# One encoder block on one core: gelu and decay steps in fewer wide VectorE instructions, the first convolution tap on ScalarE, every third low part of the weights on VectorE

## Chip, cores and metric

One core of a Trainium2 chip runs the whole block. The metric is device time in microseconds (us), the median of three runs. The names of the engines in the profile: PE is TensorE (PEld its weight loads), DVE is VectorE, ACT is ScalarE, POOL is GpSimd, SP is SyncE, which here only issues transfers.

## What is computed

The input is 256 positions of 2048 float32 features, and there is one layer. It has a mixer and a retrieval over single-neuron experts:

```python
n = rms_norm(h)
z = n @ w_in                                  # 2048 -> 4 x 1024: xr, gr, gu, gv
xc = conv(xr)                                 # depthwise, 4 taps: y = b + sum_k x[t+k] * w[k]
for each direction:                           # RG-LRU, 8 heads of 128 channels
    r, i  = sigmoid(xc @ w_a + b_a), sigmoid(xc @ w_x + b_x)
    log_a = -8 * softplus(-lam) * r
    a, u  = exp(log_a), sqrt(-expm1(2 * log_a)) * (i * xc)
    h_t   = a_t * h_{t-1} + u_t               # a scan over the 256 positions
A = gelu(gr) * (h_forward + h_backward)
B = gelu(gu) * (w_s[head] @ layer_norm(gelu(gv)) + b_s)
h = h + concat(A, B) @ w_out
h = h + peer(rms_norm(h))                     # queries, two top 16, 128 of 16384 experts a position
out = rms_norm(h)
```

Gelu is the tanh form, x (1 + tanh(GA x + GB x^3)) / 2.

## The kernel before

**Steps.** The three projections (w_in, w_out and w_q, all 2048 deep) are worked off in 256 steps in one loop, 128 for w_in, 64 for w_out and 64 for w_q. A step takes 128 rows by 512 columns of weights. The weight is split into a rounded part hi and a rest lo, and three products stand for one float32 product: hi by hi, hi by the input's lo, lo by the input's hi. `stage_h` (line 279) does the split: ScalarE casts `hi` (L286), and VectorE or GpSimd subtracts to give `lo` (L289). A counter `nl` chooses: every fourth on VectorE, except in a part of the last projection, the others on GpSimd. There are five buffers of hi and of lo. Splitting runs LH = 4 steps ahead of the matmuls. A step has 12 matmuls of 256 columns where the result stands feature by feature (w_in's groups for xr, gr and gu, and w_q), and 6 matmuls of 512 columns otherwise (w_in's groups for gv, and w_out). In this text steps are counted from 0; the groups of 16 steps of w_in come in the order xr, xr, gv, gv, gr, gr, gu, gu.

**Lanes.** All other work of the mixer stands in generators. Behind every step's matmuls, `slices` (line 80) takes one piece, up to the next yield, of the first generator in each of three lanes (`bg3`, `bg`, `bg2`). So the program's order, and with it each engine's queue, is fixed when the program is made: a yield is one step. For steps 128 to 139 slices is called twice, and `reload_x` at step 140 drains the lanes. Lane `bg3` reads finished accumulators (`lru`, `evac`), lane `bg` holds `lru2(0)` and then `lru2(1)`, lane `bg2` holds the gates in order: gate_v(0), gate_v(1), gate_r(0), gate_r(1), gate_u(0), gate_u(1). `gate_r(g)` waits, in program order, until `lru2(g)` has marked itself done.

**lru2 (line 357).** For four heads (g = 0 or 1): the convolution, per head one tensor_scalar for tap 0 with the bias (L365) and three scalar_tensor_tensor (L369), two yields a head. Then for each direction, called a decay pass here: the gate matmuls (L381) and two Tanh a head (L386, L387), Exp and Tanh a head (L394, L395), and on 1024 columns, for all four heads at once: L399 (input gate), L401 (clamp of the negated tanh), Sqrt on ScalarE (L403), twice L405 and L407 (a product and an affine step), a GpSimd product (L409), L411, and four scans (L416 or L418). After the second direction GpSimd adds the two results (L423).

**gelu2 (line 446).** Square on ScalarE (L449), a tensor_scalar (L451), a product (L453), Tanh on ScalarE (L455). It is used six times on 1024 columns, by gate_v (then L498 and the layer norm: L510 to L522), gate_r (L462, L467, then `put_y`: casts yh and rests yl, L339 and L341) and gate_u (matmuls L535 and L537 that mix the positions, L540, L544, put_y).

**What follows.** The product with w_out needs yh and yl of all lanes. After the queries come the scores, the choice of experts, and two gathers on GpSimd's queue of 256 rows each (u, then v), with the dot products (L913) and the weighted sum (L959).

Of the kernel before, what the change touches and what calls it, by code (L numbers as in the profile page):

```python
# [11 lines left out]
AF = mybir.ActivationFunctionType  # L12
OP = mybir.AluOpType
# [5 lines left out]
T = 256  # L19
# [22 lines left out]
GA = math.sqrt(2.0 / math.pi)  # L42
GB = 0.044715 * GA


def build(tc, x, mix_norm_g, w_in, conv_w, conv_b, lru_w_a, lru_b_a, lru_w_x, lru_b_x,
# [3 lines left out]
    vec, act, pool, pe = nc.vector, nc.scalar, nc.gpsimd, nc.tensor  # L50
# [19 lines left out]
    def psm(shape, name):  # L70
        return ps.tile(shape, F32, name=name, tag="m", bufs=4)
# [34 lines left out]
    G1, G2, CW, CB, BA, BX, LAM = 0, 16, 32, 64, 72, 88, 104  # L106
# [9 lines left out]
    prm = pa.tile([P, P], F32, name="prm")  # L116
# [5 lines left out]
    def wait(n):  # L122
        for _ in range(n):
            yield
# [145 lines left out]
    def load_next():  # L270
        if nload[0] < len(srcs):
            s = srcs[nload[0]]
            nload[0] += 1
            s.raw = stm.tile([P, 1024], F32, name="raw", bufs=RB)
            s.load(s.raw)

    nl = [0]

    def stage_h(s):
        if s.ahead:  # L280
            s.ahead()
        q = s.q % 2
        s.h = stm.tile([P, 512], F32R, name="hi", bufs=HB)
        s.l = stm.tile([P, 512], F32R, name="lo", bufs=HB)
        a, h, l = s.src.raw[:, q * 512:(q + 1) * 512], s.h, s.l
        act.copy(h, a)  # L286
        nl[0] += 1
        e = vec if nl[0] % 4 == 0 and not o_end + 14 <= nl[0] < o_end + 42 else pool
        e.tensor_tensor(l, a, h.bitcast(F32), op=OP.subtract)  # L289
        if s.last:  # L290
            load_next()
# [65 lines left out]
    def lru2(g, xp):  # L357
        wg = p1.tile([P, 2, 2, 4, P], F32, name="wg")
        for d in range(2):
            for n, w in enumerate((lru_w_a, lru_w_x)):  # L360
                act.dma_start(wg[:, d, n], w[0, d, 4 * g:4 * g + 4].rearrange("h c e -> c h e"))
        for b in range(4):
            hb = 4 * g + b
            o = xc[:, hb]
            vec.tensor_scalar(o, xp[:, b, 0:T], prm[:, CW + hb:CW + hb + 1], prm[:, CB + hb:CB + hb + 1],  # L365
                              op0=OP.mult, op1=OP.add)
            for k in range(1, 4):
                c = CW + 8 * k + hb
                vec.scalar_tensor_tensor(o, xp[:, b, k:k + T], prm[:, c:c + 1], o, op0=OP.mult, op1=OP.add)  # L369
                if k == 1:  # L370
                    yield
            yield
        for d in range(2):
            tr = p1.tile([P, 4, T], F32, name="ltr")
            ti = p1.tile([P, 4, T], F32, name="lti")
            zs = []
            for b in range(4 + WP):
                if b < 4:
                    z = psm([P, 2, T], "gz")
                    for n in range(2):  # L380
                        mm(z[:, n], lhsT=wg[:, d, n, b], rhs=xc[:, 4 * g + b], start=True, stop=True)  # L381
                    zs.append(z)
                if b >= WP:
                    z = zs[b - WP]
                    j = d * 8 + 4 * g + b - WP
                    act.activation(tr[:, b - WP], z[:, 0], AF.Tanh, scale=0.5, bias=drv[:, HBA + j:HBA + j + 1])  # L386
                    act.activation(ti[:, b - WP], z[:, 1], AF.Tanh, scale=0.5, bias=drv[:, HBX + j:HBX + j + 1])  # L387
                yield
            a = p1.tile([P, 4, T], F32, name="lom")
            s = p1.tile([P, 4, T], F32, name="ls")  # L390
            for b in range(4):
                j = d * 8 + 4 * g + b
                cj, ej = drv[:, C4 + j:C4 + j + 1], drv[:, C8 + j:C8 + j + 1]
                act.activation(a[:, b], tr[:, b], AF.Exp, scale=ej, bias=ej)  # L394
                act.activation(tr[:, b], tr[:, b], AF.Tanh, scale=cj, bias=cj)  # L395
                if b % 2:
                    yield

            vec.scalar_tensor_tensor(ti, ti, 1.0, xc[:, 4 * g:4 * g + 4], op0=OP.add, op1=OP.mult)  # L399
            yield  # L400
            vec.tensor_scalar(tr, tr, -1.0, 0.0, op0=OP.mult, op1=OP.max)  # L401
            yield
            act.activation(s, tr, AF.Sqrt)  # L403
            for n in range(2):
                vec.scalar_tensor_tensor(a, a, 1.0, tr, op0=OP.add, op1=OP.mult)  # L405
                yield
                vec.tensor_scalar(a, a, -1.0, 1.0, op0=OP.mult, op1=OP.add)  # L407
                yield
            pool.tensor_tensor(ti, ti, s, op=OP.mult)  # L409
            yield from wait(3)  # L410
            vec.scalar_tensor_tensor(ti, a, 1.0, ti, op0=OP.add, op1=OP.mult)  # L411
            yield
            for b in range(4):
                hb = 4 * g + b
                if d == 0:
                    vec.tensor_tensor_scan(hs[:, hb], a[:, b], ti[:, b], 0.0, op0=OP.mult, op1=OP.add)  # L416
                else:
                    vec.tensor_tensor_scan(tr[:, b][:, ::-1], a[:, b][:, ::-1], ti[:, b][:, ::-1], 0.0,  # L418
                                           op0=OP.mult, op1=OP.add)
                if b % 2:  # L420
                    yield
            if d == 1:
                pool.tensor_tensor(hs[:, 4 * g:4 * g + 4], hs[:, 4 * g:4 * g + 4], tr, op=OP.add)  # L423
                done.add(g)
            yield
# [20 lines left out]
    def gelu2(xx):  # L446

        t = p1.tile([P, 1024], F32, name="g2")
        act.activation(t, xx, AF.Square)  # L449
        yield  # L450
        vec.tensor_scalar(t, t, GB, GA, op0=OP.mult, op1=OP.add)  # L451
        yield
        vec.tensor_tensor(t, t, xx, op=OP.mult)  # L453
        yield
        act.activation(t, t, AF.Tanh)  # L455
        yield from wait(2)
        return t

    def gate_r(g, xx):
        t = yield from gelu2(xx)  # L460
        y2 = p1.tile([P, 1024], F32, name="g3")
        vec.scalar_tensor_tensor(y2, t, 1.0, xx, op0=OP.add, op1=OP.mult)  # L462
        yield
        while g not in done:
            yield
        yv = y2.rearrange("p (b t) -> p b t", b=4)
        vec.scalar_tensor_tensor(yv, yv, 0.25, hs[:, 4 * g:4 * g + 4], op0=OP.mult, op1=OP.mult)  # L467
        yield
        yield from put_y(4 * g, yv, 4)
# [528 lines left out]
    o_end = z_end + 4 * 16  # L998
# [23 lines left out]
    for n in range(N + LT):  # L1022
# [6 lines left out]
        s = steps[c]  # L1029
# [62 lines left out]
```

## Time and profile before

| what | value |
|---|---|
| three runs | 1688.69, 1699.1, 1694.52 us; median 1694.52 |
| the profiled execution | 1699.92 us, its span 1698.2 us, mean TensorE clock granted 0.747 |
| busy over the span | PE 59%, PEld 43%, DVE 77%, ACT 39%, POOL 61% |
| low parts (L289) | POOL x199, 297.0 us; DVE x57, 64.7 us |
| chain that ended last, by engine | DMA 34%, DVE 22%, PE 13%, POOL 9%, issue 7%, ACT 1% |
| read from HBM | 558.44 MB, 331 GB/s over the span |

The span runs from the first to the last instruction of the program. Busy shares are means over stages with different limits, so the stages are looked at one by one below. The granted clock is the share of TensorE's full speed; the engine has two levels, 2.4 and 1.2 GHz.

### The profile page before, as it was taken

Reading aid. Unit: us, or ns where it says so; the run is one execution under the profiler, and the core shown is the slowest. Engines: PE = TensorE matmul, PEld = TensorE weight load, DVE = VectorE, ACT = ScalarE, POOL = GpSimd, SP = SyncE. Lnnn points to the kernel's source line nnn. Section 1 sums busy time; section 2 is a strip of 40 time slices with the busy share of each in tenths; the row PEclk is TensorE's granted clock in tenths of the full one; section 3 lists DMA queues with packets and bytes.
Section 4 is the critical chain, followed back from the end, with each engine's and each line's share of the span. In section 5 each row is a group of like instructions: output and inputs, shape, how many; then the busy total and the mean of one; then the engine's idle time right before and its main releaser. Section 6 shows DMA issues by size and latency. Waiting matters only on the chain.

```text
span 1698.2 us, 14737 instructions
## 1 busy us (share of the span) xinstructions
PE 1010.1 (59%) x4352; PEld 726.2 (43%) x4352; DVE 1305.1 (77%) x1757; ACT 660.7 (39%) x1375; POOL 1029.9 (61%) x779
## 2 busy tenths in 40 slices
PE   8998899989860000000232323237799999999930
PEld 7877787779860000000121212125645555555510
DVE  6689975236698998998999998769976666666697
ACT  5564654445322111112888878878800000000002
POOL 4576874567877777777687767754444343343362
PEclk9998997999985555555555555555589999999975
DMA  6654443664879999999999999979899999999996
GB/s 201 210 157 132 133 149 107 215 222 164 298 259 385 420 420 420 420 421 420 393 420 421 419 420 420 411 308 350 262 370 408 409 410 409 409 409 410 409 412 243
DMA packets 138721, 563.62 MB, mean 332 GB/s; under 512 B 13057, under 2 KB 21393, under 8 KB 105106
## 3 DMA queue, kind: packets, MB, share of 16 engines
q0 software_dynamic: 73728, 419.46, 61.5%
q1 hardware_dynamic: 56240, 132.07, 22.0%
q10 hardware_dynamic: 8674, 11.15, 1.9%
q8 instruction: 34, 0.56, 0.1%
q14 instruction: 45, 0.37, 0.1%
HBM read 558.44 MB, written 4.19 MB: 331 GB/s over the span
## 4 chain that ended last, share of the span: by engine, by line
DMA 34%; DVE 22%; PE 13%; POOL 9%; issue 7%; ACT 1%; DVEq 0%; ACTq 0%; POOLq 0%; SPq 0%
DMA vr<-in_peer_v_dram,ids 21%; DMA row<-in_peer_u_dram,ids 12%; DVE row L913 11%; DVE acc L959 6%; PE acc_o L325 5%; POOL row L910 4%; PE acc_q L322 4%; POOL row L858 3%; POOL lo L289 2%; PE da L847 2%; DVE ah L842 1%; PE acc_z L322 1%; DMA kr<-in_peer_sub_keys_dram 1%; POOL vr L858 1%; DMA raw<-in_peer_w_q_dram 1%
## 5 line engine op out<-in xcount | busy, mean ns | idle before, releaser
L913 DVE SCALAR_TENSOR_TENSOR row<-row,xp 128x2048 f32<-128x2048 f32 x194 | 439.4, 2280 | 42.0 <-DMA row<-in_peer_u_dram,ids 35.0
L959 DVE SCALAR_TENSOR_TENSOR acc<-vr,dots,acc 128x1152 f32<-128x1152 f32 x254 | 360.6, 1420 | 142.3 <-DMA vr<-in_peer_v_dram,ids 140.3
L858 POOL DMA_INDIRECT vr<-in_peer_v_dram,ids x256 | 241.1, 942 | 303.8 <-DVE acc L959 249.1
L974 PE MATMUL sum<-raw,ht 128*128 128x448 f32 x1024 | 386.7, 540 | 0.0
L289 POOL TENSOR_TENSOR lo<-raw,hi 128x512 fp32r<-128x512 f32 x199 | 297.0, 1513 | 144.6 <-ACT hi L286 141.6
L858 POOL DMA_INDIRECT row<-in_peer_u_dram,ids x256 | 248.1, 969 | 143.1 <-DVE row L913 74.5
L847 PE MATMUL da<-ah,oh 128*128 128x128 f32 x512 | 163.4, 466 | 261.0 <-ACT ah L846 122.9
L974 PEld LDWEIGHTS sum<-raw,ht 128*128 128x128 f32 x1024 | 195.1, 191 | 191.2 <-issue 191.2
L847 PEld LDWEIGHTS da<-ah,oh 128*128 128x128 f32 x512 | 120.8, 319 | 303.7 <-ACT ah L846 148.7
L910 POOL TENSOR_TENSOR row<-row,xn 128x2048 f32<-128x2048 f32 x49 | 221.8, 4527 | 36.8 <-DMA row<-in_peer_u_dram,ids 36.4
L286 ACT CAST hi<-raw 128x512 fp32r<-128x512 f32 x256 | 153.4, 618 | 181.2 <-PE acc_o L325 48.3
L817 PE MATMUL da<-ident,dots 128*128 128x128 f32 x2 | 0.9, 448 | 295.3 <-DVE dots L919 295.3
L961 ACT COPY keep<-acc 128x1152 f32<-128x1152 f32 x2 | 2.2, 1119 | 443.3 <-DVE acc L959 443.3
L289 DVE TENSOR_TENSOR lo<-raw,hi 128x512 fp32r<-128x512 f32 x57 | 64.7, 1135 | 122.2 <-ACT hi L286 120.4
L887 ACT ACTIVATE row<-row 128x2048 f32<-128x2048 f32 x49 | 93.3, 1904 | 165.2 <-POOL row L910 165.2
L322 PE MATMUL acc_z<-xt,hi 128*128 128x256 f32 x768 | 150.1, 296 | 3.6 <-ACT hi L286 3.6
L322 PEld LDWEIGHTS acc_z<-xt,hi 128*128 128x128 f32 x768 | 126.6, 201 | 5.2 <-ACT hi L286 4.6
L817 PEld LDWEIGHTS da<-ident,dots 128*128 128x128 f32 x2 | 0.4, 184 | 295.7 <-issue 295.7
L322 PE MATMUL acc_z<-xt,lo 128*128 128x256 f32 x384 | 114.9, 299 | 14.8 <-DVE lo L289 8.0
L322 PE MATMUL acc_q<-xt,hi 128*128 128x256 f32 x512 | 100.5, 297 | 1.2 <-ACT xt L632 1.0
L823 ACT ACTIVATE oh<-oh,one 128x128 f32<-128x128 f32 x224 | 90.0, 402 | 7.3
L822 ACT ACTIVATE oh<-iota,kt 128x128 f32<-128x128 f32 x224 | 87.7, 392 | 9.7 <-PE da L847 8.6
(219 smaller groups left out, 1573.6 us busy)
## 6 DMA issues: line engine op xcount, KB each, us to landing
raw<-in_peer_v_dram SPq DMA_DIRECT2D x128, 448.0 KB, 6.8
raw<-in_w_in_dram SPq DMA_DIRECT2D x63, 512.0 KB, 4.2
raw<-in_w_out_dram SPq DMA_DIRECT2D x32, 512.0 KB, 4.1
raw<-in_peer_w_q_dram SPq DMA_DIRECT2D x32, 512.0 KB, 4.4
row<-in_peer_u_dram,ids POOLq DMA_INDIRECT x256, 13.9
vr<-in_peer_v_dram,ids POOLq DMA_INDIRECT x256, 16.5
xr<-in_x_dram ACTq DMA_DIRECT2D x2, 1024.0 KB, 8.8
hres<-h ACTq DMA_DIRECT2D x2, 1024.0 KB, 8.1
```

The lines of the kernel that those rows point to most:

```text
L286: act.copy(h, a)
L289: e.tensor_tensor(l, a, h.bitcast(F32), op=OP.subtract)
L322: mm(acc[:, c * T:(c + 1) * T], lhsT=w_[:, c * P:(c + 1) * P], rhs=a_[:, kk], start=(kk == 0 and n == 0 and c % 2 == 0), stop=fin, skip_gr ...
L822: act.activation(o, iota, AF.Abs, scale=-1.0, bias=c)
L823: act.activation(o, o, AF.Relu, scale=-1.0, bias=one)
L847: mm(tp[:, j], lhsT=o, rhs=a, start=True, stop=True)
L858: pool.indirect_dma_start(out=t, out_offset=None, in_=w, in_offset=bass.IndirectOffsetOnAxis(ap=R.ids[:, b, k:k + 1], axis=0))
L887: act.activation(t, t, AF.Copy, accum_out=d)
L910: pool.tensor_tensor(t, t, R.xn2[b], op=OP.mult)
L913: vec.scalar_tensor_tensor(t, t, 1.0, R.xn2[b] if R.late is None else in_psum(b), op0=OP.mult, op1=OP.mult, accum_out=d)
L959: vec.scalar_tensor_tensor(R.acc, t, c, R.keep[b] if k == 0 else R.acc, op0=OP.mult, op1=OP.add)
L974: mm(s, lhsT=R.ht[b][:, i], rhs=R.raws[NT + i][:, cs], start=False, stop=i == NI - 1)
```

## The change

Four edits in the mixer:

- `stage_h`: until the counter reaches the end of the w_out steps (`o_end` = 192) every third low part goes to VectorE instead of every fourth.
- `lru2`, convolution: tap 0 with the bias is an Identity activation on ScalarE with a pointer scale and a pointer bias.
- `lru2`, decay pass: the clamp is a Relu on ScalarE with scale -1, followed by Sqrt in place. The two products take the unclamped value, with the sign and the affine steps folded into their constants (a product with 1, a product with 2), so two tensor_scalar instructions (L401 and one L407) and three yields go; one tensor_scalar that adds 1 stands behind the last product.
- `gelu2`: the constant GB goes into the scale of Square, and tensor_scalar and product become one scalar_tensor_tensor; one yield goes.

```diff
@@ stage_h
-        e = vec if nl[0] % 4 == 0 and not o_end + 14 <= nl[0] < o_end + 42 else pool
+        every = 3 if nl[0] < o_end else 4
+        e = vec if nl[0] % every == 0 and not o_end + 14 <= nl[0] < o_end + 42 else pool
@@ lru2, convolution
-            vec.tensor_scalar(o, xp[:, b, 0:T], prm[:, CW + hb:CW + hb + 1], prm[:, CB + hb:CB + hb + 1],
-                              op0=OP.mult, op1=OP.add)
+            act.activation(o, xp[:, b, 0:T], AF.Identity, scale=prm[:, CW + hb:CW + hb + 1],
+                           bias=prm[:, CB + hb:CB + hb + 1])
@@ lru2, decay pass
-            vec.tensor_scalar(tr, tr, -1.0, 0.0, op0=OP.mult, op1=OP.max)
-            yield
-            act.activation(s, tr, AF.Sqrt)
-            for n in range(2):
-                vec.scalar_tensor_tensor(a, a, 1.0, tr, op0=OP.add, op1=OP.mult)
-                yield
-                vec.tensor_scalar(a, a, -1.0, 1.0, op0=OP.mult, op1=OP.add)
-                yield
+            act.activation(s, tr, AF.Relu, scale=-1.0)
+            act.activation(s, s, AF.Sqrt)
+            vec.scalar_tensor_tensor(a, a, 1.0, tr, op0=OP.add, op1=OP.mult)
+            yield
+            vec.scalar_tensor_tensor(a, a, 2.0, tr, op0=OP.add, op1=OP.mult)
+            yield
             pool.tensor_tensor(ti, ti, s, op=OP.mult)
             yield from wait(3)
-            vec.scalar_tensor_tensor(ti, a, 1.0, ti, op0=OP.add, op1=OP.mult)
+            vec.scalar_tensor_tensor(ti, a, 2.0, ti, op0=OP.add, op1=OP.mult)
+            vec.tensor_scalar(a, a, 1.0, None, op0=OP.add)
             yield
@@ gelu2
-        act.activation(t, xx, AF.Square)
-        yield
-        vec.tensor_scalar(t, t, GB, GA, op0=OP.mult, op1=OP.add)
-        yield
-        vec.tensor_tensor(t, t, xx, op=OP.mult)
+        act.activation(t, xx, AF.Square, scale=math.sqrt(GB))
+        yield
+        vec.scalar_tensor_tensor(t, t, GA, xx, op0=OP.add, op1=OP.mult)
         yield
```

## Rows read from the trace of the kernel before

**Rows 1.** Stages: length, PE PEld DVE ACT POOL busy us, clock, DMA share, GB/s.
```profile
50.00:86.60 36.60, 36.60 (x230) 33.80 (x228) 22.24 (x29) 21.60 (x38) 20.16 (x17) 0.95 0.63 192
86.60:252.40 165.80, 145.51 (x950) 132.03 (x949) 146.18 (x114) 95.18 (x161) 127.73 (x72) 0.96 0.47 143
...
293.20:381.60 88.40, 80.52 (x352) 64.78 (x350) 23.15 (x40) 39.41 (x74) 52.59 (x40) 0.96 0.64 221
...
520.00:1698.20 1178.20, 555.79 (x1550) 318.88 (x1550) 956.62 (x1315) 413.17 (x944) 686.09 (x542) 0.67 0.98 394
```

**Rows 2.** Waits from 84 to 256 us: total, times, longest.
```profile
PEld acc_z L322 <- DVE lo L289: 9.4, 7, 3.1
```

**Rows 3.** By line: count, least/median/longest in ns, first and last start in us.
```profile
L289 POOL TENSOR_TENSOR lo<-raw,hi x199: 1260/1298/3363, 6.4 to 505.2; 128x512 fp32r<-128x512 f32 x199
...
L289 DVE TENSOR_TENSOR lo<-raw,hi x57: 674/694/2878, 12.5 to 502.6; 128x512 fp32r<-128x512 f32 x57
...
L405 DVE SCALAR_TENSOR_TENSOR lom<-lom,ltr x8: 1210/2200/2315, 85.1 to 237.1; 128x1024 f32<-128x1024 f32 x8
...
L407 DVE TENSOR_SCALAR lom<-lom x8: 695/1667/2885, 87.5 to 239.4; 128x1024 f32<-128x1024 f32 x8
...
L416 DVE TENSOR_TENSOR_SCAN hs<-lom,lti x8: 660/1706/1777, 99.7 to 214.5; 128x256 f32<-128x256 f32 x8
...
L369 DVE SCALAR_TENSOR_TENSOR xc<-xp,prm,xc x24: 471/485/2497, 50.6 to 170.2; 128x256 f32<-128x256 f32 x24
...
L365 DVE TENSOR_SCALAR xc<-xp,prm x8: 397/406/1376, 50.1 to 167.7; 128x256 f32<-128x256 f32 x8
...
L423 POOL TENSOR_TENSOR hs<-hs,ltr x2: 2358/2375/2392, 146.5 to 252.3; 128x1024 f32<-128x1024 f32 x2
```

**Rows 4.** Timeline of VectorE around 100 us: start, length, instruction.
```profile
98.02 1.77 DVE L289 TENSOR_TENSOR lo<-raw,hi 128x512 fp32r<-128x512 f32 x1
99.71 5.04 DVE L416 TENSOR_TENSOR_SCAN hs<-lom,lti 128x256 f32<-128x256 f32 x3
```

**Rows 5.** Windows of single steps, the projection's instructions alone (those at the edges counted).
```profile
226.46:240.86 14.40, 14.40 (x123) 14.40 (x122) 1.22 (x1) 0.00 (x0) 1.00 0.60 191
77.08:87.96 10.88, 10.88 (x50) 9.01 (x48) 0.69 (x1) 0.00 (x0) 1.00 0.51 146
165.75:170.34 4.59, 3.56 (x25) 3.15 (x25) 0.00 (x0) 0.00 (x0) 1.00 0.25 67
```

**Rows 6.** Windows of stretches of steps: 37-48, 56-101, 112-126, 128-139, 65-68.
```profile
79.80:98.32 18.52, 16.85 (x74) 13.36 (x72) 14.94 (x10) 11.98 (x20) 15.33 (x9) 1.00 0.44 128
112.42:206.84 94.42, 78.64 (x522) 72.76 (x521) 84.87 (x73) 52.57 (x89) 69.21 (x38) 0.93 0.44 130
226.46:250.19 23.73, 22.30 (x183) 21.75 (x181) 21.06 (x14) 13.32 (x22) 21.14 (x12) 1.00 0.52 168
252.38:293.17 40.79, 39.24 (x139) 28.84 (x137) 22.61 (x21) 16.60 (x25) 17.95 (x12) 0.75 0.29 96
124.74:136.28 11.54, 8.94 (x51) 8.44 (x50) 9.94 (x7) 8.28 (x12) 7.97 (x6) 0.70 0.44 130
```

**Rows 7.** By line, ScalarE: Exp with pointer scale and bias, and Sqrt.
```profile
L394 ACT ACTIVATE lom<-ltr,drv x16: 585/592/622, 77.6 to 228.2; 128x256 f32<-128x256 f32 x16
...
L403 ACT ACTIVATE ls<-ltr x4: 1057/1060/1062, 85.6 to 232.3; 128x1024 f32<-128x1024 f32 x4
```

**Rows 8.** Timeline of ScalarE around 126 us, with idle time before and what ended it.
```profile
125.37 1.28 ACT L403 ACT_TABLE_LOAD   x1 [3.71 <-DVE ltr L401]
...
127.63 2.68 ACT L286 CAST hi<-raw 128x512 fp32r<-128x512 f32 x5
```

**Rows 9.** Chain that ended last, in order of time, from 278 to 374 us.
```profile
278.10 0.41 PE mx L535 x2
...
282.36 0.72 PE mx L535 x2
...
328.18 46.03 PE acc_o L325 x198
```

## Prediction, made before the changed kernel ran

> **What bounds the kernel now.** I read the windows by stage first, then the waits, then single stretches. The reader should see four things. (1) From 520 us to the end the DMA engines are 0.98 busy at 394 GB/s: the gathers set the pace, nothing the change touches runs there, so this 1178 us piece is only moved earlier or later [rows 1]. (2) In the input projection from 86.6 to 252.4 us TensorE is busy 145.5 of 165.8 us, so about 20 us are plain gaps; before that, from 50 to 86.6 us, it is busy all the time, and in the output projection 80.5 of 88.4 us with VectorE at 23 us [rows 1]. (3) The gaps end with a low part: weight loads alone waited 9.4 us for lo from VectorE, in seven places of up to 3.1 [rows 2]. (4) VectorE and GpSimd don't work side by side. Lo takes 0.67 us on VectorE and 1.26 on GpSimd at best, but up to 2.88 and 3.36; a scan has 0.66 at best and 1.78 at worst [rows 3]. When both are busy they alternate: three scans between lows of GpSimd take 5.04 us, 1.68 a pair, against 0.60 + 1.25 = 1.85 for the two one after the other [rows 4]. So what counts is the time of the two engines together.
>
> **A sum for that pair, tried on the kernel before.** A step of 12 matmuls of 256 columns takes TensorE 1.44 us (ten in 14.40), one of 6 matmuls of 512 columns 1.36 (eight in 10.88), and a gate matmul group adds 0.85 (two steps in 4.59) [rows 5]. Price of an instruction on the pair: its least duration [rows 3], less 0.08 by which the next one starts before it ends (98.02 + 1.77 against 99.71) [rows 4]. That gives, rounded: lo 0.60 on VectorE, 1.25 on GpSimd; a 1024-wide two-input instruction 1.13; a 1024-wide tensor_scalar 0.60; a scan 0.60; a tap 0.39, the first tap 0.31; a 1024-wide GpSimd instruction 2.4 (L423, the shortest of that kind, has 2.36). All but the lows is multiplied by 0.9, the 1.68 / 1.85 above. Casts run four steps ahead, which hides about 4 x 1.4 - 0.5 - 1.25 = 4.0 us of delay; what goes beyond is a gap. I laid the lanes' yields out step by step and summed each stretch from the step where nothing is left over to the step where the lead is last used up:
> Steps 37 to 48: lows 9 x 1.25 + 3 x 0.60 = 13.1; one decay pass 11.1 (L399 1.13, L401 0.60, two L405 2.26, two L407 1.20, L409 2.4, L411 1.13, four scans 2.4), x 0.9 = 10.0; TensorE 12 x 1.36 = 16.3. Lost: 13.1 + 10.0 - 16.3 - 4.0 = 2.8.
> Steps 56 to 101: lows 35 x 1.25 + 11 x 0.60 = 50.4; two passes 22.2, gelu and gates 10.9 (L451 and L453 three times, L498 twice, L462, L467, two yl at 0.60), L423 2.4, convolution 5.9, layer norm 8.3 (L518, L520 and L522 twice), together 49.7 x 0.9 = 44.8; TensorE 8 x 1.36 + 38 x 1.44 + 4 x 0.85 = 69.0. Lost 50.4 + 44.8 - 69.0 - 4.0 = 22.2.
> Steps 112 to 126: lows 16.8, pass, L423, L467 and a yl 15.2 x 0.9 = 13.7; TensorE 21.6. Lost 4.9.
> Sum 29.9. Measured, the three stretches take 18.52, 94.42 and 23.73 us [rows 6], less TensorE's 16.3, 69.0 and 21.6: 2.2 + 25.4 + 2.1 = 29.7. The split is coarse, the sum holds.
>
> **The change, part by part.**
> *Pair time that goes in steps 37 to 127.* Every third low part instead of every fourth: VectorE has 30 of 91 instead of 23, 7 x 0.65 = 4.6 us. Decay: one L401 and one L407 per pass, 4 x 1.20 = 4.8. Gelu: one tensor_scalar for each of four, 2.4 (the other two lie in the tail). First tap: 4 x 0.31 = 1.2. Together 13.0. The taps and passes of the first half before step 37 give nothing: TensorE has no gap there [rows 1]. Nor do the 6 more lows of the output projection, with VectorE a quarter busy.
> *But the order moves too.* A decay pass has 7 yields instead of 10, a gelu one less, so that lane ends at step 112 instead of 124. Work that lay in the last, emptier steps comes into the full ones. The same sum on the new order: steps 37 to 45, 9.3 + 0.9 x 9.9 - 12.2 - 4.0 = 2.0. Steps 55 to 93, lows 40.3, two passes 19.8, gelu and gates 8.0, L423 2.4, taps 4.7, layer norm 8.3, that is 43.2 x 0.9 = 38.9, TensorE 58.8: 16.4. Steps 103 to 114, 12.4 + 0.9 x 15.2 - 17.3 - 4.0 = 4.8. Sum 23.2. Gain 29.9 - 23.2 = **6.7**, half of the 13.0; the bounds are 0 and 13.0.
> On moving lows: the row has 0.67 against 1.26 alone [rows 3], so each moved one frees pair time. The Trainium skill (Perfetto Trace Analysis, section Optimizing Scalar/DVE Operations) says that the two engines share an SBUF read port, so that offloading between them might not help; by that, the 4.6 us would be nothing and the gain some 2.3 us smaller.
> *ScalarE's wait before Sqrt.* Now Sqrt waits for VectorE's clamp L401: 3.71 us at 125 us, and five casts stand behind it, released together at 127.63 [rows 8]. Four steps from 124.74 to 136.28 us take 11.54 [rows 6] for 5.76, lost 5.8, of which the pair's sum, followed step by step, has 2.3. With Relu on ScalarE itself that wait goes: **3.5**, bounds 0 and 5.8. Late next is Tanh of gelu, which still waits for VectorE, behind one instruction less.
> *What ScalarE gets.* Four Relu of 1024, priced as the Sqrt of that width, 1.06 each; eight taps with pointer scale and bias, as L394, 0.59 each [rows 7]: 9 us on an engine with much idle time. But now the exponentials (8 x 0.59 = 4.7 in two steps), Relu, table load (1.28) and Sqrt (3.4 together) come within three steps, with casts of 0.54 (five in 2.68) [rows 7, 8] in front of each step. Over four steps: 4 x 0.54 + 4.7 + 3.4 = 10.3 against 5.6 of TensorE, 4.7 late, with a lead of 4.0: 0.7 a pass, and more at step 84, where a gelu falls into the same steps. I charge **-2.0**; bounds 0 (TensorE is held back by the pair at these places anyway) and -6. If Relu needed a table of its own: four more loads, -5.1 on ScalarE; I take none.
> *The taps' new wait.* VectorE's second tap waits for ScalarE's first, which stands behind a cast. Behind it on VectorE stand other taps and a lo whose cast stands behind the same ScalarE work, so I charge 0; at worst a cast and a tap each for the second half, 4 x 1.2 = -4.8.
> *Tail.* From step 128 to step 140 now 40.79 us at a clock of 0.75 [rows 6], for 12 steps of 1.40 (33 in 46.03) = 16.8 plus twice 16 pairs of mixing matmuls at 0.41 = 13.1 [rows 9]: 10.9 lost. The last pass ends so late that GpSimd's sum, gate_r(1) and both gate_u come one behind another, and the pairs then run at 0.72. In the new order gate_r(1) and gate_u(0) are done by step 127 and gate_u(1) by step 134. The second mixing group starts at 0.41 and falls to 0.72 after 282 us by itself; I leave that to both groups: 6 pairs x 0.31 = 1.9, and one step behind them slower by the same ratio, 1.40 x 0.75 = 1.1, so 3.0 each. The gain is 10.9 - 6.0 = **4.9**, bounds 0 and 10.9.
> *Sum.* 6.7 + 3.5 - 2.0 + 4.9 = 13.1. The profiled execution took 1699.92 us (span 1698.2 and 1.7 around it), so it would be 1686.8. It lies 5.4 above the median of the three runs, 1694.52; from the median the forecast is **1681.4**. Everything after 381 us is taken to follow one for one, as the gathers can't start before the queries.
>
> **The rivals.**
> *All of it is collected.* All the pair's 13.0, all that is lost around the Sqrt wait 5.8, and the tail 4.9: 23.7, 1670.8. For it: the measured losses of the stretches and the tail are 29.7 + 10.9 = 40.6 us. Against it: the compressed lanes, full steps 55 to 93.
> *Only the tail.* The denser order and ScalarE's bursts eat the 10.2 of pair and Sqrt: gain 4.9, 1689.6. For it: my sum already gives half of the freed time back.
> *ScalarE becomes the bound, slower.* If the casts' lead is already used up by the pair when a pass reaches the exponentials, all 4.7 us of each pass are gaps, 19 in four passes, with the gelu's Square, load and Tanh in one of them 3.4 and the taps' waits 4.8: 27 against gains of 15.1, that is 12 us slower, 1706.4. It decides at a lead of zero at step 54, 82 or 101. Against it: ScalarE now has time between casts, and catches up at 0.54 a cast while TensorE stands. The Trainium skill (ScalarE: Activation LUTs, section Rules for kernel authors) speaks for this rival: relu, add and mul belong on VectorE rather than ScalarE. By the rows, Relu costs 1.06 there against 0.70 for a tensor_scalar on VectorE, but on an engine that nobody shares.
>
> **How the numbers follow.** Forecast 0.45, all collected 0.27, only the tail 0.21, ScalarE the bound 0.07. A measurement of this kernel tells about 1%, 16.9 us: faster means below 1677.6, slower above 1711.5. Faster: all of the first rival and a fifth of the forecast's spread, 0.36. Slower: part of the last rival, 0.03. Within 1%: 0.61. The range goes a little beyond the first rival (bounds of pair, Sqrt and tail add to 1665) and past the tail-only case to the median itself: 1667 to 1694.
>
> **What would show it.** Right: the casts' wait on L401 gone, and none of that length in its place; lo's longest times shorter; steps 56 to 101 faster by some 6 to 10 us; step 128 to 140 down to some 26 us (16.8 + 6.6 + 3.0) at a higher clock, with the first mixing group in the steps before; the stage from 520 us on as long as before. Wrong: TensorE waits for hi casts behind exponentials and Relu (last rival); the stretch from 86.6 us to step 128 as long as before in spite of shorter VectorE time (only the tail); or the time saved by 381 us is missing at the end.

## The result and the profile after

The changed kernel took 1709.55 us (median of 6 runs, 1706.13 to 1715.14), the kernel before 1697.62 (6 runs, 1688.69 to 1699.3). The ratio is 1.0073, with a 95% interval of [1.0054, 1.0091]: 12 us slower, where 13 us faster was forecast. The profiled execution took 1710.99 us, its span 1709.2, that is 11.0 more than before.

First where the time went. The start of each step's first matmul was read from both traces; lengths of stretches of steps in us:

| steps | before | after | difference | forecast |
|---|---|---|---|---|
| 0 to 24 | 51.7 | 54.1 | +2.4 | 0 |
| 24 to 37 | 21.8 | 21.8 | 0 | 0 |
| 37 to 112 | 146.7 | 150.4 | +3.8 | less |
| 112 to 140 | 66.7 | 69.7 | +3.0 | less |
| 140 to 150 | 21.0 | 24.1 | +3.1 | 0 |
| 150 to 192 | 67.4 | 67.6 | +0.2 | 0 |

These are the lengths in one execution of each kernel. 'a_keys', one of the experiments below, has the instructions of the changed kernel up to step 140, and its execution took 52.9, 21.8, 150.5 and 66.1 us in the first four stretches. So the 3.0 us of steps 112 to 140 lie within what two executions of the same instructions differ by.

From step 192 on the shift stays near 12 us. The stages, as in [rows 1], bounded by the same steps (windows of the changed kernel):

```profile
50.00:89.20 39.20, 38.09 (x241) 35.32 (x242) 21.29 (x25) 23.52 (x42) 17.51 (x15) 0.96 0.60 195
89.20:276.06 186.86, 157.06 (x982) 140.55 (x980) 142.03 (x117) 107.19 (x178) 118.95 (x67) 0.93 0.43 129
302.46:394.21 91.75, 79.88 (x352) 64.39 (x350) 26.10 (x42) 37.62 (x72) 47.20 (x36) 0.95 0.63 214
531.55:1709.20 1177.65, 555.18 (x1550) 318.84 (x1550) 957.05 (x1315) 413.18 (x944) 688.00 (x542) 0.67 0.98 394
```

The last line is the gathers: 1177.65 us at a DMA share of 0.98, against 1178.20 before. That stage only moved, as forecast. In the second line TensorE has 29.8 us of gaps, against 20.3 before, though VectorE and GpSimd have less to do. (The first mixing group now lies in this line; before it lay in the next stage.) The stretches of [rows 6], steps 37 to 48, 56 to 101, 112 to 126 and 128 to 139:

```profile
82.37:104.45 22.08, 18.79 (x81) 14.63 (x80) 18.46 (x11) 13.56 (x22) 16.74 (x10) 1.00 0.45 128
115.97:213.45 97.48, 79.36 (x538) 72.88 (x537) 85.48 (x74) 61.83 (x105) 64.44 (x37) 0.96 0.46 138
232.78:274.62 41.84, 37.61 (x215) 33.12 (x213) 22.61 (x20) 14.18 (x22) 20.92 (x14) 0.76 0.34 110
276.06:302.46 26.40, 26.40 (x107) 20.19 (x105) 9.91 (x13) 11.78 (x18) 10.63 (x8) 0.87 0.35 118
```

The last line, steps 128 to 139, fell from 40.79 to 26.40 us; the forecast said some 26. But what left them stands in the third line, 41.84 against 23.73. And steps 56 to 101, which were to be 6 to 10 us faster, take 97.48 us against 94.42. Two new prices came out as assumed, a third did not (by line: least/median/longest ns, first and last start):

```profile
L366 ACT ACTIVATE xc<-xp,prm x8: 595/600/602, 56.7 to 152.5; 128x256 f32<-128x256 f32 x8
L402 ACT ACTIVATE ls<-ltr x4: 1052/1054/1055, 86.3 to 220.2; 128x1024 f32<-128x1024 f32 x4
L411 DVE TENSOR_SCALAR lom<-lom x4: 1652/1658/1672, 98.0 to 234.0; 128x1024 f32<-128x1024 f32 x4
```

A tap on ScalarE 0.60 (0.59 assumed), Relu 1.05 (1.06), and Relu brought no table load of its own. Only the one tensor_scalar left in a pass never ran at its 0.70 of [rows 3]: it meets GpSimd each time and takes 1.66. Now the waits from 86.57 us to step 118 at 245.42 (total, times, longest):

```profile
POOL lo L290 <- ACT hi L286: 42.7, 19, 7.6
DVE lo L290 <- ACT hi L286: 28.0, 8, 5.9
...
PEld acc_z L323 <- POOL lo L290: 17.6, 11, 3.5
...
ACT yh L340 <- DVE g L465: 15.2, 2, 9.3
...
PEld acc_z L323 <- DVE lo L290: 7.8, 4, 2.4
```

The same view of the kernel before, up to its step 118 at 235.10 us:

```profile
POOL lo L289 <- ACT hi L286: 27.9, 12, 5.0
DVE lo L289 <- ACT hi L286: 17.3, 8, 6.2
...
PEld acc_z L322 <- POOL lo L289: 8.3, 12, 2.4
PEld acc_z L322 <- DVE lo L289: 7.3, 5, 3.1
...
ACT L403 <- DVE ltr L401: 6.2, 2, 3.7
```

ScalarE's wait for the clamp is gone, as forecast. In its place ScalarE waits 15.2 us in two places at L340, the cast of the gated result, for the gate on VectorE (L465). Before there was one such wait, 9.6 us long, but it ended at 257 us, beside the first mixing group; now one of 5.9 ends at 195 us and one of 9.25 at 244 us, in the full steps. And the two engines that make low parts now wait for ScalarE's hi cast 42.7 and 28.0 us, before 27.9 and 17.3; the weight loads wait 17.6 and 7.8 us for low parts, before 8.3 and 7.3. ScalarE from 215 to 246 us shows two places where casts come late (start, length, instruction, idle time before):

```profile
215.44 1.04 ACT L453 ACTIVATE g<-g 128x1024 f32<-128x1024 f32 x1
...
219.17 1.12 ACT L286 CAST hi<-raw 128x512 fp32r<-128x512 f32 x2
220.19 1.05 ACT L402 ACTIVATE ls<-ltr 128x1024 f32<-128x1024 f32 x1
221.27 1.28 ACT L403 ACT_TABLE_LOAD   x1
222.56 1.06 ACT L403 ACTIVATE ls<-ls 128x1024 f32<-128x1024 f32 x1
223.53 2.68 ACT L286 CAST hi<-raw 128x512 fp32r<-128x512 f32 x5
...
234.35 0.62 ACT L286 CAST hi<-raw 128x512 fp32r<-128x512 f32 x1 [0.83 <-PE acc_z L323]
244.23 0.62 ACT L340 CAST yh<-g 128x512 fp32r<-128x512 f32 x1 [9.25 <-DVE g L465]
244.75 1.13 ACT L286 CAST hi<-raw 128x512 fp32r<-128x512 f32 x2
```

From 213.15 to 223.53 the exponentials, gelu's Tanh, Relu, the load and Sqrt leave room for three casts; then five come at once, as they did behind the clamp in [rows 8]. At 244.23 the gate's cast has held up the hi casts behind it for 9.25 us. TensorE at that point:

```profile
243.17 0.39 PE L323 MATMUL acc_z<-xt,lo 128*128 128x256 f32 x1 [1.76 <-POOL lo L290]
...
245.42 0.79 PE L323 MATMUL acc_z<-xt,hi 128*128 128x256 f32 x2 [0.80 <-ACT hi L286]
247.12 0.58 PE L323 MATMUL acc_z<-xt,lo 128*128 128x256 f32 x1 [0.90 <-POOL lo L290]
...
249.55 0.79 PE L533 MATMUL mx<-bs,ones 1*128 1x128 f32 x2
250.27 0.80 PE L535 MATMUL mx<-wsT,vv 128*128 128x128 f32 x2
...
260.39 0.80 PE L535 MATMUL mx<-wsT,vv 128*128 128x128 f32 x2
260.84 0.77 PE L323 MATMUL acc_z<-xt,hi 128*128 128x256 f32 x2
```

Steps 116 and 117 take 2.5 and 4.4 us instead of 1.44. From step 116 to the mixing group TensorE stops four times, 0.77 us at 239.71 and the three times above, and only the last two, 0.80 and 0.90 us, come behind the gate's cast. The 1.76 us ended with a low part that stood on GpSimd behind its sum of the two directions, for which GpSimd had waited 2.37 us:

```profile
239.15 2.75 POOL L423 TENSOR_TENSOR hs<-hs,ltr 128x1024 f32<-128x1024 f32 x1 [2.37 <-DVE ltr L418]
241.86 1.25 POOL L290 TENSOR_TENSOR lo<-raw,hi 128x512 fp32r<-128x512 f32 x1
```

Then the first mixing group, now behind the matmuls of step 118, runs 16 pairs of 0.72 us, 11.3 us. Windows of the time before and of the group:

```profile
236.00:245.40 9.40, 6.09 (x47) 5.48 (x45) 7.12 (x8) 1.17 (x3) 4.74 (x3) 1.00 0.35 104
245.42:261.00 15.58, 14.68 (x45) 10.80 (x46) 7.77 (x5) 4.13 (x7) 6.66 (x4) 0.50 0.35 119
```

TensorE was busy 6.09 of 9.40 us at a granted clock of 1.00, and from 245.42 us it is granted 0.50, the 1.2 GHz level. That is not fixed by the order. In 'a_keys' every engine was busy for the same times ahead of the group, and then the clock stayed up longer:

```profile
234.95:244.35 9.40, 6.09 (x47) 5.48 (x45) 7.12 (x8) 1.17 (x3) 4.74 (x3) 1.00 0.34 101
244.38:255.36 10.98, 9.79 (x45) 7.23 (x46) 7.76 (x5) 4.01 (x7) 6.66 (x4) 0.86 0.51 168
```

There 4 of the 16 pairs took 0.72 us, and step 118 with the group 10.8 us, against 15.4 in the changed kernel's own profile. What made the clock fall earlier in the one is not shown. The last new loss lies ahead of step 147:

```profile
320.20 1.11 PE L663 MATMUL kt<-ident,kr 128*128 128x128 f32 x4 [7.78 <-DMA kr<-in_peer_sub_keys_dram]
```

TensorE waits 7.78 us for the keys, which were asked for at 303.44; before it waited 3.15. It came to them 10.0 us after the start of step 140, before 10.4. So nearly all of the difference is the load itself, which landed later after its issue (start and length, before and after):

```profile
294.13 12.48 DMA kr<-in_peer_sub_keys_dram
```

```profile
303.44 16.71 DMA kr<-in_peer_sub_keys_dram
```

### The profile page after: what moved, and what is told of

The parts are those of the page before. It is cut to its first block, busy times and chain, and to the rows that moved or that the text cites. A ratio compares the mean times of both kernels' runs of the same rounds, so it can differ in the third digit from the quotient of the medians.

```text
span 1709.2 us, 14715 instructions
## 1 busy us (share of the span) xinstructions
PE 1008.5 (59%) x4352; PEld 727.0 (43%) x4352; DVE 1290.8 (76%) x1751; ACT 667.7 (39%) x1387; POOL 1009.5 (59%) x763
## 4 chain that ended last, share of the span: by engine, by line
DMA 33%; DVE 24%; PE 14%; POOL 9%; issue 7%; ACT 1%; ACTq 0%; POOLq 0%; DVEq 0%
DMA vr<-in_peer_v_dram,ids 20%; DVE row L911 12%; DMA row<-in_peer_u_dram,ids 11%; DVE acc L957 6%; PE acc_o L326 5%; PE acc_q L323 4%; POOL row L908 4%; POOL row L856 3%; POOL lo L290 2%; PE acc_z L323 2%; DVE ah L840 2%; PE da L845 1%; DMA kr<-in_peer_sub_keys_dram 1%; POOL vr L856 1%; DMA raw<-in_peer_w_q_dram 1%
## 5 line engine op out<-in xcount | busy, mean ns | idle before, releaser
L290 POOL TENSOR_TENSOR lo<-raw,hi 128x512 fp32r<-128x512 f32 x183 | 270.9, 1497 | 187.1 <-ACT hi L286 176.0
L290 DVE TENSOR_TENSOR lo<-raw,hi 128x512 fp32r<-128x512 f32 x73 | 74.0, 1018 | 147.9 <-ACT hi L286 147.6
```

## The experiments

Each run has its own runs of the kernel before on the same chip, so the ratios are what to compare. The ratio on record is not always the quotient of the two medians: they lie up to 0.2% apart (0.9952 and 0.9933 for 'pad_late'), and a difference between two runs that is smaller than that decides little. The right part is the length of the stretches of steps in the run's one profile, in us. Besides the pair above, 'pad_late' and 'late_keys' have the same instructions up to step 140: 135.7 and 138.0 us for steps 37 to 112, 65.8 and 62.9 for 112 to 140.

| run | median us | ratio, 95% | 0-24 | 37-112 | 112-140 | 140-150 |
|---|---|---|---|---|---|---|
| before | 1697.62 | 1 | 51.7 | 146.7 | 66.7 | 21.0 |
| changed | 1709.55 | 1.0073 [1.0054, 1.0091] | 54.1 | 150.4 | 69.7 | 24.1 |
| u_tap | 1712.31 | 1.0076 [1.0057, 1.0095] | 54.2 | 153.1 | 68.7 | 22.4 |
| u_lo | 1703.64 | 1.0038 [1.0018, 1.0058] | 49.5 | 148.4 | 71.6 | 17.1 |
| u_decay | 1697.61 | 0.9996 [0.9979, 1.0013] | 52.2 | 143.8 | 66.3 | 18.7 |
| pad | 1691.42 | 0.9951 [0.9933, 0.9969] | 55.6 | 136.9 | 65.8 | 19.3 |
| p_relu | 1703.99 | 1.0031 [1.0010, 1.0051] | 54.4 | 143.6 | 71.6 | 25.8 |
| p_prod | 1703.24 | 1.0038 [1.0018, 1.0058] | 53.3 | 146.1 | 72.4 | 22.6 |
| pad_vclamp | 1693.83 | 0.9978 [0.9965, 0.9991] | 51.3 | 138.5 | 67.0 | 19.3 |
| pad_late | 1688.25 | 0.9952 [0.9937, 0.9967] | 50.2 | 135.7 | 65.8 | 19.2 |
| a_late | 1707.48 | 1.0060 [1.0037, 1.0083] | 51.3 | 153.6 | 68.9 | 24.4 |
| a_keys | 1702.44 | 1.0037 [1.0022, 1.0052] | 52.9 | 150.5 | 66.1 | 14.8 |
| p_decay | 1686.75 | 0.9944 [0.9927, 0.9961] | 54.0 | 138.4 | 64.4 | 18.6 |
| late_keys | 1681.11 | 0.9915 [0.9889, 0.9941] | 50.4 | 138.0 | 62.9 | 14.9 |
| p_front | 1694.75 | 0.9969 [0.9951, 0.9986] | 53.4 | 143.1 | 65.9 | 18.4 |
| p_end | 1701.76 | 1.0018 [1.0005, 1.0032] | 52.3 | 147.7 | 65.0 | 21.5 |
| b_lo | 1702.87 | 1.0035 [1.0018, 1.0051] | 54.1 | 147.2 | 67.8 | 17.3 |
| decay_keys | 1679.53 | 0.9887 [0.9870, 0.9905] | 51.0 | 138.4 | 61.4 | 14.4 |
| decay4 | 1684.58 | 0.9921 [0.9894, 0.9949] | 50.3 | 139.9 | 63.8 | 16.5 |
| decay4_keys | 1684.91 | 0.9930 [0.9905, 0.9954] | 49.9 | 139.9 | 65.3 | 14.4 |

**Which part of the change.** Four kernels, each the changed one with one thing undone. 'u_decay' has the decay pass of before (its instructions and its ten yields), 'u_lo' every fourth low part, 'u_tap' the first tap on VectorE. 'pad' keeps all new instructions and puts back the four yields that went with the old ones:

```diff
+            yield
             act.activation(s, tr, AF.Relu, scale=-1.0)
             act.activation(s, s, AF.Sqrt)
             vec.scalar_tensor_tensor(a, a, 1.0, tr, op0=OP.add, op1=OP.mult)
             yield
+            yield
             vec.scalar_tensor_tensor(a, a, 2.0, tr, op0=OP.add, op1=OP.mult)
             yield
+            yield
...
         vec.scalar_tensor_tensor(t, t, GA, xx, op0=OP.add, op1=OP.mult)
         yield
+        yield
```

> The changed kernel with its yields put back (10 in a decay pass, one more in gelu), so that every piece stands in the step that it had in the kernel before; the shorter instructions stay. The changed kernel takes 1709.6 us, 12 more than before. If the order is the cause (the same work in fewer steps, so that exponentials, Relu and Sqrt hold up the casts), this one is faster than before by the pair's 7 to 13 us: 1685 to 1691. If the lows on VectorE are the cause, the order changes little: 1704 to 1712. If the waits for the taps are, 1702 to 1712.

> The changed kernel with the decay pass of before (clamp on VectorE, two more wide instructions, 10 yields). Order theory: most of the loss is in this edit, 1690 to 1697. Lows or taps theory: about as the changed kernel or a little slower, since VectorE has 4.8 us more, 1707 to 1716.

> The changed kernel with every fourth low part on VectorE again. Order theory: the lows free pair time, so without them it is slower or the same, 1709 to 1714. Lows theory (a low part on VectorE stands behind wide instructions, and TensorE waits for it): 1694 to 1702.

> The changed kernel with tap 0 on VectorE again. Order theory: within 3 us of the changed kernel, 1707 to 1713. Taps theory (VectorE waits for ScalarE's tap behind casts, and ScalarE has eight more activations): 1698 to 1704.

'pad' is 18 us faster than the changed kernel and faster than before, by yields alone. 'u_tap' changes nothing: the tap and its wait are out. 'u_decay' takes back 0.8%, 'u_lo' 0.35%, which lies between its two forecasts.

**Which of the yields.** 'p_relu' has only the first of the yields above, 'p_prod' only the two behind the products. 'p_decay' has these three and not gelu's.

> Changed kernel with one yield put back in each decay pass, ahead of Relu. If it is ScalarE's burst (exponentials, then Relu, table load and Sqrt with no step between) that holds the casts up, this yield alone gives back most of the 18 us that the four yields together gave: 1693 to 1700 us. If it is the work of VectorE and GpSimd that lies too close (the products, the gelu), it gives back little: 1704 to 1710.

> Changed kernel with one yield put back behind each of the two products of a decay pass, none ahead of Relu. The reverse of the run before: by the burst of ScalarE 1703 to 1709 us; by the density of VectorE's and GpSimd's work 1693 to 1700. If only the length of the lane counts (where its last work falls against the casts), both runs are near each other and two yields give about twice what one gives.

> The changed kernel with the three yields of the decay pass put back, the gelu's not. If the yields of the decay pass are what counts (one gave 0.42%, two 0.35%, all four 1.2%): 1693 to 1697 us. If the length of the lane counts whatever work it lies behind, the gelu's (seven times, three of them ahead of step 112) weighs as much as the others and it is 1697 to 1701.

'p_relu' and 'p_prod' each came out where the one yield or the two give back little: 0.42 and 0.35%. So neither the burst of ScalarE nor the density of the products is the cause by itself. Together the three give 1.29%, more than the sum, and 'p_decay' is faster than both of its ranges; gelu's gives nothing measurable beside them. In steps 37 to 112 the single gains nearly add up: 6.8 and 4.3 us, together 12.0. What the single runs lack lies in steps 112 to 150, which take them 97.4 and 95.0 us and 'p_decay' 83.0 (the profiles of the two single runs took 5.3 and 4.5 us more than their medians, so part of this may be chance): in the single runs the first mixing group still lies ahead of step 128 or at its edge. The windows of 'p_decay' for steps 37 to 112 and 112 to 140, the changed kernel's under them:

```profile
82.00:220.40 138.40, 123.40 (x787) 110.71 (x786) 108.68 (x94) 93.57 (x157) 96.62 (x56) 0.99 0.50 149
220.40:284.77 64.37, 61.40 (x330) 51.19 (x329) 41.52 (x36) 31.53 (x49) 35.91 (x21) 0.87 0.37 119
```

```profile
82.37:232.78 150.41, 124.84 (x788) 111.64 (x786) 122.08 (x98) 99.12 (x165) 99.95 (x56) 0.98 0.45 134
232.78:302.46 69.68, 65.45 (x331) 54.75 (x329) 33.17 (x33) 26.57 (x41) 32.22 (x22) 0.80 0.35 115
```

In steps 37 to 112 VectorE is busy 122.08 us with 98 instructions in the changed kernel, 108.68 with 94 in 'p_decay'. The four more are wide ones of the last decay pass, which falls into these steps there; at the means of their lines they make up some 7.8 of the 13.4 us. The other 5.6 us are the same instructions taking longer, as L411 above does beside GpSimd.

**Close together, or shifted.** The three yields can be put where they leave the middle of a pass dense. 'p_front' puts them ahead of the exponentials, 'p_end' behind the scans:

```diff
+            yield from wait(3)
             a = p1.tile([P, 4, T], F32, name="lom")
```

```diff
                 if b % 2:
                     yield
+            yield from wait(3)
             if d == 1:
                 pool.tensor_tensor(hs[:, 4 * g:4 * g + 4], hs[:, 4 * g:4 * g + 4], tr, op=OP.add)
```

> The changed kernel with the three yields of a decay pass put ahead of the exponentials, not between Relu and the products: the lane is as long as in 'p_decay', its middle as dense as in the changed kernel. If the length of the lane counts (what the later work of the lane meets), about as 'p_decay': 0.993 to 0.997. If the density of the pass counts, about as the changed kernel: 1.004 to 1.009.

> The changed kernel with the three yields put behind the scans of each decay pass: same length, dense from the exponentials to the scans. By the length of the lane 0.993 to 0.997, by the density 1.004 to 1.009. If the mixing's meeting with the last steps of the projection were all (steps 112 to 150 lost 7 us against the kernel before), 1.000 to 1.003, with steps 37 to 112 as slow as in the changed kernel (150.4 us).

'p_front' keeps Relu behind the exponentials and the products one step apart, and still has four fifths of what 'p_decay' has (1.04 of 1.29%). In steps 112 to 150 it has nearly all (84.3 us against 83.0 and 93.8), in steps 37 to 112 7.3 of 12.0. So most of the loss is where the lanes' work falls, the smaller part (4.7 us) how close it lies within a pass. By the quotients of the medians (0.9987 against 0.9942) it is two thirds, and the yields of 'p_front' also part the gates' Tanh from the exponentials on ScalarE, so length and density are not wholly separated. 'p_end' has only 0.55%: it leaves the first pass of each half where the changed kernel has it, and steps 37 to 112 stay slow (147.7). Its nearest forecast, that the mixing's place were all, gave 1.000 to 1.003.

**The clamp.** 'pad' with the clamp on VectorE again, one line:

```diff
-            act.activation(s, tr, AF.Relu, scale=-1.0)
+            vec.tensor_scalar(s, tr, -1.0, 0.0, op0=OP.mult, op1=OP.max)
```

> The four yields as in 'pad', but the clamp ahead of Sqrt on VectorE as before the change, so that ScalarE waits for it. The prediction gave 3.5 us to the removed wait (0 to 5.8), and the clamp takes 4 x 0.6 us of VectorE: by that 1694 to 1698 us, and ScalarE's wait on that line is back with several us. If the wait had only been one that hid another, 1691 to 1693.

The wait is back (waits from 84 to 250 us):

```profile
ACT ls L404 <- DVE ls L403: 6.9, 4, 2.4
```

The ratio rises from 0.9951 to 0.9978, 4.6 us, and the stretches from 37 to 140 by 2.8 us; but the quotients of the medians, 0.9964 and 0.9966, hardly differ, and 1693.83 us lies between the two forecasts. No step lies between clamp and Sqrt here, as one did before the change, so the wait is not quite the old one. That Relu on ScalarE pays is likely, its size is not shown. The Trainium skill (ScalarE: Activation LUTs, section Rules for kernel authors) would keep it on VectorE; no run here shows a gain from that, and the ratio speaks against it.

**The low parts.** 'a_late' and 'pad_late' take every third low from the 24th on only; 'b_lo' is the kernel before with every third, and nothing else.

```diff
-        every = 3 if nl[0] < o_end else 4
+        every = 3 if 24 <= nl[0] < o_end else 4
```

> The changed kernel with every third low part on VectorE only from the 24th on, every fourth before. If the third lows cost the first 24 steps some 3 us (step 24 started 2.6 us later than before in the changed kernel, 4.0 in 'pad', but 0.5 earlier in 'pad_vclamp', 2.2 earlier with every fourth): 1704 to 1707 us, step 24 at -2 to 0, and what is left against 1703.6 of 'u_lo' is the price of the moved lows after step 24, next to nothing. If the lateness of step 24 was only chance, 1709 to 1710.

> The four yields as in the run 'pad', and every third low part only from the 24th on, every fourth before. If the lows of the first steps take VectorE away from the small set-up work that the first steps wait for (4.0 us later at step 24 in 'pad'), that is back: 1686 to 1689 us, step 24 within 1 us of the kernel before. If the lows there cost nothing and the lateness has another cause, 1691 as 'pad'.

> The kernel before with every third low part on VectorE and nothing else. The prediction gave the moved lows 4.6 us of the pair's time, half of it collected: 0.998 to 0.999, steps 37 to 112 shorter by 1 to 4 us. If VectorE is the one of the two engines that ends last in the full steps, they cost time: 1.001 to 1.004.

Every third instead of every fourth moves 16 low parts to VectorE (73 instead of 57), two of them in the first 24 steps. By themselves they cost 0.35%, in the old order ('b_lo') as in the new ('u_lo'). Part of it is in the first 24 steps. They take 51.3 to 55.6 us in the twelve profiles with every third low there, 53.5 in the mean, and 49.5 to 51.7 in the eight with every fourth, 50.5 in the mean: 3.0 us. Single profiles overlap, and the medians don't resolve it ('a_late' 0.13% better, 'pad_late' no better in ratio, though 0.3% by the quotients of the medians). What in these steps is late was not settled: in the changed kernel TensorE waits 3.3 us for the load of the mixing's weights there, before 2.0. From the 24th on the lows gave nothing in steps 37 to 112 of 'b_lo' (147.2 against 146.7). Where the rest of the 0.35% lies was not found.

**The keys.** On ScalarE's queue the reload of x, 2 MB, stands ahead of the keys. 'a_keys' is the changed kernel with the keys first, 'late_keys' is 'pad_late' with the same edit:

```diff
         for b in range(NT):
             h1.append(pa.tile([P, D], F32, name="h1%d" % b, tag=("xc", "hs")[b]))
             xr.append((pa, p1)[b].tile([P, D], F32, name="xr%d" % b, tag="x%d" % b))
-            act.dma_start(xr[b], x2[b * P:(b + 1) * P, :])
...
             act.dma_start(R.kr[n], peer_sub_keys[0].rearrange("h p n k -> n (h p) k")[:, 8 * n:8 * n + 8])
+        for b in range(NT):
+            act.dma_start(xr[b], x2[b * P:(b + 1) * P, :])
```

> The changed kernel with the two loads of the keys issued ahead of the reload of x on the same queue instead of behind it. Step 147 took 10.1 us in the changed kernel, 5.5 before, 1.4 without a wait. If the keys are late because 2 MB of x lie in front of them, step 147 falls to 1.4 to 3 us and the whole by 7 to 9: 1701 to 1703 us. If the loads of the weights take the DMA engines whatever the order, or x is now late for the residual, 1707 to 1710.

> All that gave something, in one kernel: the four yields, every third low from the 24th on, the keys ahead of x. The run 'pad_late' took 1688.3 with 1699.7 for the kernel before on its chip (0.995). Step 147 waits little there already, so the keys' order gives 0 to 4 us: ratio 0.992 to 0.995, the fastest so far. If the keys' order collides with the reload of x for the residual, 0.995 or more.

Steps 140 to 150 take 14.4 to 14.9 us in all four kernels with the keys first, and 16.5 to 25.8 in all others: the wait is gone, at no visible price for x. In the ratio it gave 0.36% in the changed kernel and 0.37% to 'late_keys'.

**The best version.** 'decay_keys' is 'p_decay' with the late lows and the keys first; 'decay4' is 'p_decay' with every fourth low, 'decay4_keys' the same with the keys first.

> The three yields of the decay pass, every third low from the 24th on, keys ahead of x, no yield in the gelu. 'p_decay' had 0.9944 and 'late_keys' 0.9915; the gelu's yield made no difference in sum (0.9944 against 0.9951). So 0.989 to 0.993, that is 1678 to 1685 us with about 1697 before. If the gelu's yield matters with the other two edits in, 0.993 or more.

> The three yields of the decay pass with every fourth low part on VectorE throughout, as before the change. 'p_decay' had 0.9944. If the third lows cost 0.35% in every order: 0.991. If they pay in the padded order, where VectorE has room, as the prediction's sum says: 0.995 to 0.998. If only the first 24 steps count: 0.992 to 0.993.

> The same with the keys ahead of x; against 'decay_keys' (0.9887) it differs by the lows from the 24th on alone. If those cost time as in the changed kernel (about 0.2%): 0.986 to 0.988, the fastest. If they pay in the padded order: 0.990 to 0.992.

'decay_keys' is the fastest, 1679.5 us, 1.1% below the kernel before. Its keys don't hold TensorE up:

```profile
289.04 0.60 PE L667 MATMUL kt<-ident,kr 128*128 128x128 f32 x4
```

Against 'decay4_keys' it differs by the lows from the 24th on alone, 14 of them on VectorE, and is 0.43% faster (four times of 1678.4 to 1681.1 us against four of 1683.5 to 1687.3): in this order they pay, where they gave nothing in the old. In steps 37 to 112 both kernels with these lows take 138.4 us ('p_decay', 'decay_keys'), both without 139.9. The Trainium skill (Perfetto Trace Analysis, section Optimizing Scalar/DVE Operations) says that offloading between VectorE and GpSimd might not help; 'b_lo' agrees with that (1.0035), 'decay_keys' against 'decay4_keys' does not. 'decay4' against 'decay4_keys' shows no gain from the keys (0.9921 and 0.9930): its own wait was only some 2 us, less than the intervals.

## Why the prediction was wrong

**The step that failed is "the order moves too".** The prediction saw that a lane with fewer yields ends earlier, and charged it by the sum of VectorE's and GpSimd's time: gain 6.7 instead of 13.0, a price of 6.3. With the yields put back, steps 37 to 112 take 136.9 us ('pad') instead of 150.4, so the new order costs 13.5 there. The gain itself was real, but smaller than summed: in the old order 9.8 us (146.7 - 136.9) against 13.0 + 3.5 - 2.0 = 14.5. The moved lows, 4.6 of the 13.0, are one part that did not show ('b_lo'). So 9.8 less 13.5 stands where 8.2 was forecast; the rest of the miss is the tail, the first 24 steps and the keys, below.

**Where the sum was blind.** In the stretches that it named for the new order, steps 37 to 45, 55 to 93 and 103 to 114, it had losses of 2.0 + 16.4 + 4.8 = 23.2 us. Measured, less TensorE's time in the prediction, they are 3.3 + 22.1 + 4.9 = 30.4, as much as its stretches lost in the kernel before (29.7). And behind them, where by the sum nothing was left over, steps 94 to 102 take 19.3 us and steps 115 to 117 8.3, against 13.0 and 4.3 of TensorE's time (13.7 and 4.3 in 'pad'): 10.3 us more. In both places a wait at L340 ends (5.9 and 9.25 us), with casts behind it in ScalarE's order, and a total of two engines' time can't show that. But it is not all of it: of TensorE's stops from step 116 on, 2.5 us came ahead of the gate's cast and 1.7 behind it, and steps 93 to 102, 22.9 us here and 15.1 in 'pad', still take 19.0 in 'p_decay' and 21.6 in 'p_end', which have no such wait there. What this wait costs stays open; no run takes it away alone.

**The tail, 4.9.** Steps 128 to 139 fell to 26.4 as forecast, with the first mixing group in the steps before. But steps 112 to 140 gained nothing: 69.7 us in the changed kernel and 66.1 in 'a_keys' with the same instructions, against 66.7 before. The forecast let six pairs of each group run at 0.72 and the rest at 0.41. In the first group it was 13 of 16 before, all 16 in the changed kernel, 4 in 'a_keys'; so the rise by 3.0 is no effect of the order that one profile could show, and neither is the gain of 2.3 in 'p_decay', where that group stands behind step 128. What the order did cost in both profiles is the 4.0 us of steps 116 and 117, which the moved work takes from TensorE there.

**Not in the sum at all.** The lows of the first 24 steps were given no cost, since TensorE has no gap from 50 us on; in the changed kernel it has 1.1 us of gaps there, and the rest lies ahead of 50 us. And steps 140 to 150, 3.1 us more: the keys' load, which stands behind x on its queue, landed 16.7 us after its issue instead of 12.5. Why it took longer is not shown. The prediction took the output projection to follow one for one.

**Right:** the wait for the clamp goes (its size, 3.5 with bounds 0 to 5.8, is not settled: 'pad_vclamp' costs 4.6 us by the ratio, with the clamp's own time in it, and next to nothing by the medians); steps 128 to 139; the taps at nothing; Relu's price and no table of its own; the stage of the gathers unchanged. Not seen: shorter low parts (the longest take 2.89 us on VectorE and 3.34 on GpSimd, before 2.88 and 3.36).

**The rivals.** "ScalarE becomes the bound" came nearest (1706.4), and it has something for it: casts do come late behind exponentials, Relu and Sqrt. But the yield that parts them gave only 0.42% ('p_relu'), and with the burst kept whole 'p_front' recovers 1.04%. So that its number is near is in part luck. It was named at 4.7 us in each pass; the loss is rather one of place, and the chance of 0.07 was too small for any way in which the order alone makes the kernel slower.

**Open:** which of the shifted meetings costs what in steps 37 to 112 (the pass with gelu, the gate's cast, GpSimd's sum, the products with GpSimd's lows), why the clock fell earlier in one profile than in another, and why the first 24 steps are later with more lows on VectorE.

## What to carry to other kernels

Where lanes are interleaved by yields, an instruction that goes takes its yield with it and moves everything behind it: first keep the order (leave the yield in), measure, and only then close the gap. A sum of engine times tells what can be gained, not what is; beside it look for each instruction of an in-order engine that waits for another lane and has the critical casts behind it. Before a stretch of one profile is explained, look at a second profile of the same instructions: here two of them differed by 3.6 us in steps 112 to 140, mostly by the granted clock. And look at what stands ahead of an urgent load on its queue: here 2 MB of another load did, and it was a wait before and after.

## What the runs showed of the hardware that was not expected

The same 1024-wide tensor_scalar on VectorE took 0.70 us at best before and never less than 1.65 in the changed kernel, where it always met GpSimd's work: VectorE's instructions take longer when they fall together with GpSimd's (some 5.6 us over steps 37 to 112, changed kernel against 'p_decay'). The same mixing matmuls behind the same 9.40 us of work, with the same busy times of all engines, ran at a granted clock of 0.50 in one profile and 0.86 in another: the prediction had taken the course of the second group in one profile [rows 9] for the rule. And the order of two loads on one queue made a difference of 9.3 us in TensorE's time (steps 140 to 150, 24.1 in the changed kernel and 14.8 in 'a_keys').
